# One more seven-product block in the first FFN slab pair that has any, and in each sweep of the FFN's last product

## The chip, the cores and the metric

The kernel is one program on one core of a Trainium2 chip. The metric is device time in microseconds (us); lower is better. Engines are named as in the profile: PE (matrix products), DVE (elementwise), ACT (elementwise and functions), POOL and SP (here mostly issuers of DMA). "Lnnn" is a line of the kernel.

## The reference

One decoder layer for 256 rows of width 2048, all in fp32:

```python
mod = silu(c) @ ada_w + ada_b          # six vectors: sh1, sc1, g1, sh2, sc2, g2
h   = rms_norm(x) * (1 + sc1) + sh1
u, lru_gate, q, k, v, mix_gates = split(h @ w_in + b_in)
y_lru  = rg_lru(conv(u)) * gelu(lru_gate)
y_attn = sliding_window_attention(q, k, v, sinks)
merged = gate_lru * (y_lru @ w_lru_out) + gate_attn * (y_attn @ w_attn_out)
x  = x + g1 * (merged @ w_o)
h2 = rms_norm(x) * (1 + sc2) + sh2
gate, up = split(h2 @ w_ffn_in)        # hidden size 5632
x  = x + g2 * ((silu(gate) * up) @ w_ffn_out)
out = rms_norm(x) * final_g
```

## The kernel before

**Products.** Every weight is read once, in 512 KB tiles `raw` of 128x1024. A weight tile is split in two: ACT casts it to `hi` (L330), DVE subtracts, `lo = raw - hi` (L342). A product of fp32 accuracy is then three matmuls, hi x hi, lo x hi and hi x lo (`mm3`, L382 to L384; in the plain blocks of the last sweeps L1391).

**Items.** All weights of the layer stand in one list, `items`, one tile each. `step(i)` does the products of item i; ahead of them it issues, for later items, the load of item i+5 (SP's queue; five `raw` buffers), `hi` of item i+3 (four buffers) and `lo` of item i+2 (three buffers). Whatever else DVE and ACT have to do (the posts of a finished block, the steps of side jobs) is written between these by a planner that keeps an estimated clock. The order on each engine is thus fixed when the program is built.

**Quads: plain and seven.** A quad is a pair of k-tiles (2 x 128 rows of the weight) by 1024 output columns. Done plainly it is two items and 24 matmuls. `seven()` does the same quad as a 2x2 block product with seven products instead of eight, 21 matmuls and four items: two raw tiles of it (here l0, of which half is used, and l1), and two sums of weight blocks, `wx` and `wy`. `wx` is loaded by POOL (`fill`, two DMAs of 256 KB, L443) and then a second block is added to it by two accumulating DMAs (`add`, L447); `step(i)` issues the fill for item i+15 and the add for item i+10. `wy` is two DVE additions (L458, L459). The seven products go to PSUM banks that all sevens of a slab or sweep share (`p`, `q`, `r`, `u`) and to the banks of the plain results. When the last of them is done, DVE adds the shared banks into the result.

The activations need sums as well. For the FFN's first product the sums of x are made in `second_norm` (`hs`, L477 to L480, L1186). For the second they are made slab by slab in `f_parts` (L1228; `fc` and `fs` for a slab that has a k-tile pair in `SEVEN`, `parts_of` with `fl`, L991, for one that has none), and in the sweep `al` is subtracted from them (`parts_low`, L1409).

**The stages that the change touches**, in order of time:
- `w_o`, four slabs of 512 columns, whose last post (`o_post`, L1120 to L1122) ends in the second RMSNorm;
- FFN in: 11 slab pairs (gate and up, 512 columns each) of eight quads. Slab pair 0 is plain, the others have sevens at the places that a string of turns gives ("7" is a seven, "-" a plain quad), at the k-tiles `SEVEN_1`;
- FFN out, sweep 1 (`w_f2a`, output columns 0 to 1023; k-tiles 0 to 35 by `TURNS`, then eight plain k-tiles) and sweep 2 (`w_f2d`, columns 1024 to 2047; k-tiles 0 to 35). `SEVEN` lists the k-tiles at which a sweep has a seven. After sweep 2 the last eight k-tiles of columns 1024 to 2047 follow in eight more items, and the residual, the second half of the final norm and the stores (`late`, L1461 to L1575).

**A side job.** `ada` makes the modulation vectors: SP loads a tile `aw`, DVE multiplies and sums it (L532). `ada_to(3, 4)` runs it until sh2 and sc2 are complete. `hold_sides` sets the planner's slack so low that no side job runs until `second_norm` is written.

Of the kernel before, what the change touches and what calls it, by code (L numbers as in the profile page):

```python
# [64 lines left out]
N_MADE, N_HOLD = 5, 4  # L65

N_SUM = (16, 11)
SEVEN = tuple(range(6, 36, 4))

SEVEN_1, SLAB_7 = (4, 6, 10, 12), 1  # L70

SLAB_G = 4
TURNS_1 = {1: "---7-77-"}

TURNS = "--7-7-7-7-7-7-7-7-"
EARLY = NH - 2 * N_HOLD

N_SPARE = 5
# [5 lines left out]
def hybrid_layer(  # L84
# [21 lines left out]
    def b4(name, dt=F32, shape=(4, S)):  # L106
        used["b4"] += 1
        return bp.tile([P, *shape], dt, tag="b4", name=name)
# [6 lines left out]
    def sum_bank(name):  # L115
        return ps.tile([P, 512], F32, tag="bank", name=name)
# [178 lines left out]
    items = []  # L295
# [397 lines left out]
    for i in range(N_PIECES):  # L693
        for n in range(N_F if i == 0 else 0, len(START)):
            s, k0, k1 = START[n], ends[i][n], ends[i + 1][n]
# [8 lines left out]
    def ada_to(*ms):  # L704
        while not {(m, kt) for m in ms for kt in range(NK)} <= cols_done:
            if not ada.advance():
                clock["pe"] += 1
                halves.fetch()
# [339 lines left out]
    def load_rows(s):  # L1048
        def before():
            xr.append(b4(f"xr{s}", F32, (2, 512)))  # L1050
            nc.sync.dma_start(xr[s], x_r[:, s * 512:(s + 1) * 512].rearrange("(t p) n -> p t n", p=P))
            if s == 3:
                ada_to(3, 4)
        return before

    def keep_rows(s):
# [29 lines left out]

    def hold_sides():

        clock["slack"] = -1e9
        return 0, 0  # L1090

    items[-2].before.append(hold_sides)

    def turn(p, of_w=False):

# [132 lines left out]
    def f_parts(s, pts):  # L1228

        seven_ = [j for j in range(2) if 4 * s + 2 * j in SEVEN]  # L1230
        if not seven_:
# [22 lines left out]
    def add_pair(s):  # L1254
# [54 lines left out]
        start = len(items)  # L1309
        turns = TURNS_1.get(s, "--77-77-")  # L1310
        sevens = SEVEN_1[:turns.count("7")]
# [43 lines left out]
    def bank(t, n):  # L1355

        if (t, n) not in fin:
            fin[t, n] = sum_bank(f"pf{t}{n}")
        return fin[t, n]
# [39 lines left out]
    def seven_last(k, n, src):  # L1399
        parts = {}  # L1400

        def parts_high():
            hi = parts[0] = b4(f"ah{n}_{k}", F32R, (8, P))
            nc.scalar.copy(hi[:, 0:7, :], f_sum[k][:, 0:7, :])
            return 0, 0.9

        def parts_low():
            lo = parts[1] = b4(f"al{n}_{k}", F32R, (8, P))
            nc.vector.tensor_tensor(lo[:, 0:7, :], f_sum[k][:, 0:7, :], f32(parts[0][:, 0:7, :]), op=ALU.subtract)  # L1409
            return 1.0, 0  # L1410

        def own(to):
            if to not in "pqru":
                return bank(int(to[0]), n + int(to[1]))
            if k == SEVEN[0]:
                fin[to] = sum_bank(f"p{to}{n}")
            return fin[to]

        items[-3].before.append(parts_high)
        items[-2].before.append(parts_low)  # L1420
        seven(
            (src[k], src[k + 1]), lambda j, i: src[k + j][:, i * 512:(i + 1) * 512], True,
            lambda a: [parts[h][:, a, :] for h in range(2)], own, k == SEVEN[0], k == SEVEN[-1],
            (lambda: combined(n)) if k == SEVEN[-1] else None,
        )

    def combined(n):

        v = [b4(f"v{n}{i}", F32, (2, 512)) for i in range(2)]
        pq, pqu, pqr, pqur = v[0][:, 0, :], v[0][:, 1, :], v[1][:, 0, :], v[1][:, 1, :]  # L1430
        nc.scalar.copy(pq, fin["p"])

        def add(t, j, x):
            y = sp.tile([P, 512], F32, tag="t2", name=f"yv{n}{t}{j}")
            x2 = x2_of(t, (n + j) * 512, (n + j + 1) * 512)
            nc.vector.tensor_tensor(y, x, g2_of((n + j) * 512, (n + j + 1) * 512), op=ALU.mult)
            nc.vector.tensor_tensor(x2, y, x2, op=ALU.add)

        yield 0, 0.6
        add(0, 0, pq)  # L1440
        nc.vector.tensor_tensor(pq, fin["q"], pq, op=ALU.add)
        yield 1.8, 0
        nc.vector.tensor_tensor(pqu, fin["u"], pq, op=ALU.add)
        nc.vector.tensor_tensor(pqr, fin["r"], pq, op=ALU.subtract)
        nc.vector.tensor_tensor(pqur, fin["r"], pqu, op=ALU.subtract)
        yield 1.8, 0
        add(0, 1, pqr)
        yield 1.2, 0
        add(1, 0, pqu)
        yield 1.2, 0  # L1450
        add(1, 1, pqur)
        free(b4=2)
        yield 1.2, 0
        if n == 2:
            yield from early_rows()
# [38 lines left out]
    for n, src in ((0, w_f2a), (2, w_f2d)):  # L1494
        start = len(items)
        kinds = {"7": iter(SEVEN), "-": iter(k for k in range(0, EARLY, 2) if k not in SEVEN)}
        turns = [next(kinds[c]) for c in TURNS]
        for k in turns + list(range(EARLY, NH if n == 0 else EARLY, 2)):
            if k in SEVEN:
                seven_last(k, n, src)  # L1500
# [244 lines left out]
```

## Time and profile before

| what | value |
|---|---|
| time, median of 3 runs | 1537.02 us (1536.7 to 1537.57) |
| the profiled execution: its own time | 1538.73 us |
| its span, first to last instruction | 1537.0 us |
| mean granted TensorE clock | 0.998 |
| busy: PE / DVE / ACT / POOL | 99% / 89% / 57% / 11% of the span |
| DMA | 444.58 MB, mean 289 GB/s |

The span is what the trace covers; the time of the same execution is 1.73 us longer. In the trace a row gives the start of an instruction in us from the span's start, its duration, its engine and line, and, in square brackets, how long the engine sat idle before it and what ended that. Durations of instructions that follow each other overlap a little, since the ends are drawn with the pipeline's latency; what an instruction costs its engine is the distance from its start to the next one's.

### The profile page before, as it was taken

The numbers are of one execution on the slowest core, as the hardware profiler recorded it, in microseconds if no ns is written. First come the engines' busy times: TensorE is split into PE (matmuls) and PEld (weight loads), VectorE is DVE, ScalarE is ACT, GpSimd is POOL, SyncE is SP. The second block draws the span as 40 slices with busy tenths as digits, with TensorE's granted clock in tenths as the row PEclk, the third lists the DMA queues.
The fourth block names the chain that finished last, engine by engine and source line by source line (L and its number), as shares of the span: only waits on it lengthen the run. The fifth ranks groups of instructions, "written<-read, shape, count | busy, mean of one in ns | idle before, by whom it ended". The sixth has DMA issues, their size and how long they took to land.

```text
span 1537.0 us, 20204 instructions
## 1 busy us (share of the span) xinstructions
PE 1521.0 (99%) x6851; PEld 1249.0 (81%) x6851; DVE 1365.3 (89%) x1835; ACT 880.7 (57%) x1142; POOL 163.5 (11%) x232
## 2 busy tenths in 40 slices
PE   8999999999999999999999999999999999999997
PEld 5788888888888787888887878888888888888886
DVE  7999999888898888988988899999999999888987
ACT  4654444886964446444444556656665556664664
POOL 0000000000000000000002231034212122321200
PEclk9999999999999999999999999999999999999999
DMA  9999988656786887999999999589898979989983
GB/s 368 383 345 362 345 315 301 207 181 217 241 286 226 291 308 283 364 325 341 377 373 347 312 338 273 167 254 332 274 273 248 269 243 298 288 257 297 275 266 124
DMA packets 138440, 444.58 MB, mean 289 GB/s; under 512 B 16064, under 2 KB 16224, under 8 KB 138336
## 3 DMA queue, kind: packets, MB, share of 16 engines
q1 hardware_dynamic: 113056, 384.02, 70.2%
q0 software_dynamic: 24992, 58.75, 16.1%
q8 instruction: 53, 0.87, 0.2%
q10 hardware_dynamic: 288, 0.52, 0.1%
q14 instruction: 51, 0.42, 0.1%
HBM read 439.02 MB, written 4.21 MB: 288 GB/s over the span
## 4 chain that ended last, share of the span: by engine, by line
PE 93%; DMA 3%; DVE 3%; ACT 0%; issue 0%; SPq 0%; DVEq 0%; ACTq 0%
PE pf L1391 10%; PE f L383 6%; PE f L382 6%; PE f L384 6%; PE wi L383 6%; PE wi L384 6%; PE wi L382 6%; PE wl L384 2%; PE wl L383 2%; PE wga L384 2%; PE wl L382 2%; PE wga L382 2%; PE wgl L383 2%; PE wga L383 2%; PE wgl L384 2%; PE wa L384 2%
## 5 line engine op out<-in xcount | busy, mean ns | idle before, releaser
L330 ACT CAST hi<-raw 128x1024 fp32r<-128x1024 f32 (+1 forms) x540 | 532.3, 996 | 419.1 <-PE wi L384 87.4
L342 DVE TENSOR_TENSOR lo<-raw,hi 128x1024 fp32r<-128x1024 f32 (+1 forms) x540 | 611.9, 1149 | 82.1 <-issue 37.7
L383 PE MATMUL wi<-lo,h 128*128 128x512 f32 x432 | 168.4, 390 | 3.3 <-DVE lo L342 3.3
L382 PE MATMUL wi<-hi,h 128*128 128x512 f32 x432 | 169.9, 393 | 0.0
L384 PE MATMUL wi<-hi,h 128*128 128x512 f32 x432 | 168.2, 389 | 0.0
L382 PE MATMUL f<-hi,h 128*128 128x512 f32 x406 | 158.8, 391 | 0.0
L383 PE MATMUL f<-lo,h 128*128 128x512 f32 x406 | 158.1, 389 | 0.0
L384 PE MATMUL f<-hi,h 128*128 128x512 f32 x406 | 158.0, 389 | 0.0
L532 DVE CUSTOM_DVE_ANT_0 aw<-aw,crow,vec 128x1024 f32<-128x1024 f32 x95 | 120.5, 1277 | 6.0 <-DMA aw<-in_ada_t_dram 6.0
L532 DVE CUSTOM_DVE_ANT_0 aw<-aw,crow,modc 128x1024 f32<-128x1024 f32 x95 | 121.1, 1277 | 1.6 <-DMA aw<-in_ada_t_dram 1.6
L330 ACT CAST hi<-wy 128x1024 fp32r<-128x1024 f32 x55 | 58.0, 1055 | 74.3 <-PE f L384 32.1
L383 PEld LDWEIGHTS wi<-lo,h 128*128 128x128 f32 x432 | 81.1, 188 | 20.9 <-DVE lo L342 4.3
L342 DVE TENSOR_TENSOR lo<-wx,hi 128x1024 fp32r<-128x1024 f32 x55 | 67.2, 1222 | 32.4 <-issue 28.5
L330 ACT CAST hi<-wx 128x1024 fp32r<-128x1024 f32 x55 | 58.0, 1055 | 64.8 <-PE pf L1391 24.0
L382 PEld LDWEIGHTS wi<-hi,h 128*128 128x128 f32 x432 | 81.1, 188 | 16.8 <-ACT acc L611 0.2
L384 PEld LDWEIGHTS wi<-hi,h 128*128 128x128 f32 x432 | 81.1, 188 | 16.7
L384 PEld LDWEIGHTS f<-hi,h 128*128 128x128 f32 x406 | 76.2, 188 | 15.8
L383 PEld LDWEIGHTS f<-lo,h 128*128 128x128 f32 x406 | 76.2, 188 | 15.7 <-DVE lo L342 0.3
L382 PEld LDWEIGHTS f<-hi,h 128*128 128x128 f32 x406 | 76.2, 188 | 15.6
L447 POOL DMA_DIRECT2D wx<-in_w_f_dram x78 | 69.8, 969 | 79.5 <-DMA wx<-in_w_f_dram 78.4
L443 POOL DMA_DIRECT2D wx<-in_w_f_dram x78 | 44.7, 627 | 287.6 <-DVE lo L342 95.2
L342 DVE TENSOR_TENSOR lo<-wy,hi 128x1024 fp32r<-128x1024 f32 x55 | 67.2, 1222 | 6.9 <-ACT hi L330 4.3
(347 smaller groups left out, 3094.1 us busy)
## 6 DMA issues: line engine op xcount, KB each, us to landing
aw<-in_ada_t_dram SPq DMA_DIRECT2D x190, 512.0 KB, 6.7
raw<-in_w_in_dram SPq DMA_DIRECT2D x164, 512.0 KB, 5.1
raw<-in_w_f_dram SPq DMA_DIRECT2D x137, 512.0 KB, 6.5
wx<-in_w_f_dram POOLq DMA_DIRECT2D x156, 256.0 KB, 7.9
raw<-in_w_f2a_dram SPq DMA_DIRECT2D x36, 512.0 KB, 6.4
raw<-in_w_lru_dram SPq DMA_DIRECT2D x32, 512.0 KB, 4.6
raw<-in_w_att_dram SPq DMA_DIRECT2D x32, 512.0 KB, 5.5
raw<-in_w_o_dram SPq DMA_DIRECT2D x32, 512.0 KB, 8.1
```

What stands on the lines that cost most here:

```text
L330: nc.scalar.copy(hi[:, cs], live[i][0][:, cs])
L342: nc.vector.tensor_tensor(lo[:, cs], raw[:, cs], f32(hi[:, cs]), op=ALU.subtract)
L382: nc.tensor.matmul(ps, lhsT=lh, rhs=rh, start=start, stop=False, skip_group_check=True)
L383: nc.tensor.matmul(ps, lhsT=lh, rhs=rl, start=False, stop=False, skip_group_check=True)
L384: nc.tensor.matmul(ps, lhsT=ll, rhs=rh, start=False, stop=stop, skip_group_check=True)
L443: nc.gpsimd.dma_start(x[:, j * 512:(j + 1) * 512], block(0, 1))
L447: nc.gpsimd.dma_start(got["x"][:, j * 512:(j + 1) * 512], block(j, j), accum_op=ALU.add)
L532: nc.vector.tensor_tensor_reduce(out=r, in0=r, in1=crow[j], op0=ALU.mult, op1=ALU.add, scale=1.0, scalar=dst if j else vec[:, v:v + 1], ac ...
L1391: nc.tensor.matmul(bank(t, n), lhsT=l[:, rows(t)], rhs=w[:, c0:c0 + 512], start=kt == 0 and k == 0, stop=kt == (EARLY - 2 if (t, n) == (1, ...
```

## The change

Three constants change, and the call `ada_to(3, 4)` with the place of `hold_sides`:

```diff
-SEVEN = tuple(range(6, 36, 4))
+SEVEN = tuple(range(2, 36, 4))
 
 SEVEN_1, SLAB_7 = (4, 6, 10, 12), 1
...
-TURNS_1 = {1: "---7-77-"}
-
-TURNS = "--7-7-7-7-7-7-7-7-"
+TURNS_1 = {}
+
+TURNS = 9 * "-7"
...
             nc.sync.dma_start(xr[s], x_r[:, s * 512:(s + 1) * 512].rearrange("(t p) n -> p t n", p=P))
-            if s == 3:
-                ada_to(3, 4)
         return before
...
     def hold_sides():
 
+        ada_to(3, 4)
         clock["slack"] = -1e9
         return 0, 0
 
-    items[-2].before.append(hold_sides)
+    items[-3].before.append(hold_sides)
```

- **Slab pair 1** had three sevens of eight quads, in the turns `---7-77-`; without an entry in `TURNS_1` it gets the turns that slab pairs 2 to 10 have, `--77-77-`, with four.
- **Each sweep** had eight sevens of 18 quads and has nine. A sweep now begins plain, seven and ends with a seven (of its k-tiles 0 to 35), where it began plain, plain, seven and ended with a plain quad. The new seven is at k-tiles 2 and 3, so slab pair 0 now makes `fc` and `fs` in `f_parts` instead of `fl`.
- **`ada_to(3, 4)`** stood at the first item of the last `w_o` slab; it now stands at that slab's last item but two, in `hold_sides`, one item earlier than `hold_sides` was.

What this does to the order of instructions shows at three places. First, DVE at the end of `w_o`. `lo_6925` to `lo_6964` are the splits of the first tiles of FFN in, `aw` is a step of `ada`, and `yo` begins the last post of `w_o`. Before:

```order
L532 ISA aw_6864,modc<-aw_6864,crow_108,vec 128x1024
...
L342 TENSOR_TENSOR lo_6925<-raw_6858,hi_6902 128x1024
L532 ISA aw_6886,modc<-aw_6886,crow_108,vec 128x1024
...
L342 TENSOR_TENSOR lo_6946<-raw_6880,hi_6923 128x1024
L342 TENSOR_TENSOR lo_6964<-raw_6900,hi_6944 128x1024
L1120 TENSOR_TENSOR yo_7008<-wo_0_0_6821,g_6095 128x512
```

After (the numbers in the names shift by one, the lines too):

```order
L532 ISA aw_6864,modc<-aw_6864,crow_108,vec 128x1024
...
L342 TENSOR_TENSOR lo_6925<-raw_6858,hi_6902 128x1024
L342 TENSOR_TENSOR lo_6945<-raw_6880,hi_6923 128x1024
L342 TENSOR_TENSOR lo_6963<-raw_6900,hi_6943 128x1024
L1119 TENSOR_TENSOR yo_7007<-wo_0_0_6821,g_6095 128x512
```

The step `aw_6886` has left this place; it stands some 40 rows further down, in FFN in. Second, POOL's queue from the same time on, with the `wx` tiles of slab pair 1. Before:

```order
L443 DMA wx_7291<-in_w_f1_dram 128x512 x2
L447 DMA wx_7291<-in_w_f1_dram 128x512 x2
L443 DMA wx_7432<-in_w_f1_dram 128x512 x2
L443 DMA wx_7542<-in_w_f1_dram 128x512 x2
L447 DMA wx_7432<-in_w_f1_dram 128x512 x2
```

After:

```order
L443 DMA wx_7246<-in_w_f1_dram 128x512 x2
L443 DMA wx_7339<-in_w_f1_dram 128x512 x2
L447 DMA wx_7246<-in_w_f1_dram 128x512 x2
L447 DMA wx_7339<-in_w_f1_dram 128x512 x2
L443 DMA wx_7479<-in_w_f1_dram 128x512 x2
```

Two fills now stand ahead of the first add. Third, DVE at the start of sweep 2, where the residual of sweep 1 (`y` and `x`, four pairs) is worked off between the splits. Before:

```order
L1461 TENSOR_TENSOR y_0_12264<-pf_11293,g_12033 128x512
...
L342 TENSOR_TENSOR lo_12271<-raw_12207,hi_12248 128x1024
L1461 TENSOR_TENSOR y_0_12289<-pf_11301,g_12033 128x512
...
L342 TENSOR_TENSOR lo_12295<-raw_12228,hi_12269 128x1024
L1461 TENSOR_TENSOR y_512_12311<-pf_11295,g_12033 128x512
...
L342 TENSOR_TENSOR lo_12317<-raw_12246,hi_12293 128x512
L1409 TENSOR_TENSOR al_6_12321<-fs_7918,ah_6_12297 128x896
L1461 TENSOR_TENSOR y_512_12335<-pf_11303,g_12033 128x512
...
L458 TENSOR_TENSOR wy<-wx,raw_12267 128x512
```

After:

```order
L1460 TENSOR_TENSOR y_0_12298<-pf_11312,g_12082 128x512
...
L342 TENSOR_TENSOR lo_12303<-raw_12244,hi_12280 128x512
L1408 TENSOR_TENSOR al_2_12307<-fs_7537,ah_2_12284 128x896
L1460 TENSOR_TENSOR y_0_12325<-pf_11320,g_12082 128x512
...
L458 TENSOR_TENSOR wy<-wx,raw_12262 128x512
...
L342 TENSOR_TENSOR lo_12336<-raw_12262,hi_12301 128x1024
L1460 TENSOR_TENSOR y_512_12353<-pf_11314,g_12082 128x512
...
L342 TENSOR_TENSOR lo_12361<-wx,hi_12334 128x1024
L1460 TENSOR_TENSOR y_512_12367<-pf_11322,g_12082 128x512
...
L342 TENSOR_TENSOR lo_12375<-wy,hi_12359 128x1024
```

The first seven's half split, `al` and `wy` now stand among the residual pairs, where two whole splits of plain tiles stood (the second row of each pair is left out above).

## The prediction

> **What bounds the kernel now.** First the page's busy times and its shares of the chain that ended last:
>
> ```profile
> PE 1521.0 (99%) x6851; PEld 1249.0 (81%) x6851; DVE 1365.3 (89%) x1835; ACT 880.7 (57%) x1142; POOL 163.5 (11%) x232
> PE 93%; DMA 3%; DVE 3%; ACT 0%; issue 0%; SPq 0%; DVEq 0%; ACTq 0%
> ```
>
> PE is the bound nearly everywhere, so fewer matmuls are a gain of their full length. But DVE is at 89% over the whole span, and a seven takes matmuls from PE by giving DVE sums. So the question at each place is whether DVE, or a DMA before it, is then still in time. Next the chain itself, in order of time (start, us):
>
> ```profile
> 809.21 13.02 DMA raw<-in_w_f_dram
> 822.32 1.06 ACT hi L330
> 823.44 1.11 issue
> 824.54 0.70 DVE yo L1120
> ...
> 1298.32 5.44 PE pf L1391 x24
> 1303.77 0.87 PE ft L982 x8
> 1304.64 5.46 PE pf L1391 x24
> 1314.86 5.44 PE pf L1391 x24
> ...
> 1386.26 38.08 PE pf L1391 x168
> ...
> 1500.49 21.76 PE pf L1391 x96
> ```
>
> A plain quad is 24 matmuls in 5.44 us, 0.2267 each; 168 of them in 38.08 give the same. The chain leaves PE where w_o joins FFN in (809 to 824): there a load that took 13 us, its cast, and a post of DVE set the time. In the sweeps it runs on PE without a break.
>
> **Arithmetic.** One seven more in slab pair 1 and one more in each sweep: three quads of 21 matmuls instead of 24, 9 x 0.2267 = **-2.04 us**. This is all that the change can win by matmuls, 0.13%. Under 0.2% (3.07 us) this kernel's measurement can't tell a difference from none; so faster or slower is decided by the waits at five places.
>
> **Place 1, the join of w_o and FFN in.** DVE, ACT and POOL there:
>
> ```profile
> 820.63 1.28 DVE L532 CUSTOM_DVE_ANT_0 aw<-aw,crow,vec 128x1024 f32<-128x1024 f32 x1 [2.02 <-DMA aw<-in_ada_t_dram]
> ...
> 823.40 1.23 DVE L342 TENSOR_TENSOR lo<-raw,hi 128x1024 fp32r<-128x1024 f32 x1 [0.34 <-ACT hi L330]
> ```
>
> ```profile
> 824.88 1.05 ACT L330 CAST hi<-raw 128x1024 fp32r<-128x1024 f32 x1 [1.51 <-DMA raw<-in_w_f_dram]
> 825.99 0.63 ACT L1122 ACTIVATE yo<-xr 128x512 f32<-128x512 f32 x1
> ```
>
> ```profile
> 812.86 1.08 POOL L443 DMA_DIRECT2D wx<-in_w_f_dram  x2 [93.06 <-PE wo L384]
> ...
> 823.51 1.12 POOL L443 DMA_DIRECT2D wx<-in_w_f_dram  x2 [1.08 <-PE wo L384]
> ```
>
> The step `aw` at 820.63 is the one that moves away. It buys nothing: the last split before the post (823.40) waits for the cast at 822.32, and that for the load issued at 809.21. DVE idles 0.34 us before it already, and would only idle longer. The step's own 1.21 us fall due in FFN in (place 2).
>
> On POOL a second fill now stands ahead of the first add. Before, POOL reached it at 823.51, held by the end of w_o. After, its buffer is one that w_o's last slab gives back two items after the first fill's: 812.86 + 2 x 2.72 (half a plain quad) = 818.3. So 512 KB are asked for 5 us earlier. What such a fill does to the loads in flight, by the DMA queues from 817 to 820 us (first fill under way) and from 821 to 824 (none):
>
> ```profile
> q1 hardware_dynamic: 203, 0.75, 61.6%
> q0 software_dynamic: 140, 0.47, 39.2%
> ```
>
> ```profile
> q1 hardware_dynamic: 336, 1.22, 102.2%
> ```
>
> SP's loads (q1) get 0.75 MB in 3 us beside POOL's queue (q0), and 1.22 MB alone. The Trainium skill ("DMA: Bandwidth & Descriptors", Queues, rings and completion order) says that each DMA engine takes turns between the queues it has work for, a packet at a time; the trace agrees, with 39% and 62%. The first fill was issued at 812.86 and moved most of its 0.5 MB from 817 on, some 4 us later; the second, issued at 818.3, would move from 822.3. It then meets the load that ended at 824.88 (the cast's idle of 1.51 us ended with it): 2.6 us at 0.75/1.22 instead of full rate, about 1.0 us lost. ACT casts that tile directly before the squares of the norm (L1122, 825.99), which are on the path to h2. So 0 (if its packets come after 824.9) to +1.4 us; I take **+1.0**.
>
> **Place 2, slab pair 1.** Durations on DVE, and DVE's waits there:
>
> ```profile
> 874.04 1.22 DVE L342 TENSOR_TENSOR lo<-raw,hi 128x1024 fp32r<-128x1024 f32 x1
> ...
> 880.06 1.23 DVE L342 TENSOR_TENSOR lo<-raw,hi 128x1024 fp32r<-128x1024 f32 x1 [1.08 <-ACT hi L330]
> ...
> 890.92 0.68 DVE L458 TENSOR_TENSOR wy<-wx,raw 128x512 f32<-128x512 f32 x1
> ...
> 892.25 0.68 DVE L342 TENSOR_TENSOR lo<-raw,hi 128x512 fp32r<-128x512 f32 x1
> 892.85 1.28 DVE L532 CUSTOM_DVE_ANT_0 aw<-aw,crow,modc 128x1024 f32<-128x1024 f32 x1
> ...
> 894.06 0.28 DVE L477 TENSOR_TENSOR hs<-x1T 128x128 f32<-128x128 f32 x1
> ...
> 894.99 1.22 DVE L342 TENSOR_TENSOR lo<-wx,hi 128x1024 fp32r<-128x1024 f32 x1
> 896.12 1.22 DVE L342 TENSOR_TENSOR lo<-wy,hi 128x1024 fp32r<-128x1024 f32 x1
> ```
>
> ```profile
> 895.81 0.39 PE L382 MATMUL fr<-hi,hs 128*128 128x512 f32 x1
> 896.26 0.50 PE L383 MATMUL fr<-lo,hs 128*128 128x512 f32 x1
> 896.60 0.40 PE L384 MATMUL fr<-hi,hs 128*128 128x512 f32 x1
> ```
>
> ```profile
> 890.00:910.00 20.00, 19.93 (x88) 15.89 (x87) 18.99 (x26) 11.05 (x13) 8.79 (x13) 1.00 1.07 309
> ```
>
> By distances of starts a split costs 1.13 us (894.99 to 896.12), a half split 0.60, `wy` 1.33 (890.92 to 892.25), an `ada` step 1.21, four `hs` sums 0.93. A plain quad is then 2.26 us of DVE, a seven 0.60 + 1.33 + 3 x 1.13 = 5.32, against 4.76 us of PE (21 x 0.2267): a seven alone already outruns PE. From 890 to 910 DVE is busy 18.99 of 20 us (third pair of numbers after the window's length), and PE already waits for the split of `wx` (895.81 to 896.60 is 0.79 us for two steps of 0.227, 0.34 lost; some 0.9 in the whole slab pair).
>
> The change adds to DVE +3.06 (5.32 - 2.26), +1.21 (the moved step), and +0.3 since slab pair 0's post makes `fc` and `fs` (0.60 + 0.93) instead of two `fl` (1.2). The first seven starts one quad earlier, before DVE has any lead. Counting on from 874.04 in the order of the changed kernel, with the wait for the raw tile at 880.06 kept, DVE ends the split of the first `wx` at 892.1; PE wants it at 890.6, so it waits 1.5. The same count gives 0.5, 0.5, 1.1 and 0.3 at the next tiles of the two sevens: 3.9 in place of 0.9, **+3.0**. Bounds: +0.9 if the loads come 1 to 2 us earlier than in the trace (the idle of 1.08 is then DVE's to use), +4.5 if they come later by the 0.5 MB more that a seven loads (0.5 MB is 1.2 us at 1.22 MB in 3 us).
>
> **Place 3, start of sweep 1**, and **place 4, start of sweep 2**, on DVE:
>
> ```profile
> 1301.87 2.95 DVE L342 TENSOR_TENSOR lo<-raw,hi 128x1024 fp32r<-128x1024 f32 x3
> 1304.75 1.08 DVE L1409 TENSOR_TENSOR al<-fs,ah 128x896 fp32r<-128x896 f32 x1
> ...
> 1411.91 0.69 DVE L1461 TENSOR_TENSOR y<-pf,g 128x512 f32<-128x512 f32 x1 [0.31 <-PE pf L1391]
> ...
> 1413.24 1.22 DVE L342 TENSOR_TENSOR lo<-raw,hi 128x1024 fp32r<-128x1024 f32 x1
> ```
>
> Sweep 1: DVE is occupied with the last slab's post until 1301.87. Now no second plain quad (5.44 PE, 2.26 DVE) comes before the seven: half split 0.60, `al` 1.0, `wy` 1.33, split 1.13, two more splits, and only then the two `fl` of the last slab (0.60 each), to 1309.4. The seven's products `u` and `q` go to banks that hold the last slab's transposes until these `fl`. So the seven, which could run from 1304.64 to 1309.40, ends at 1310.9: **+1.5** (0 if the banks turn out free, +2 if the raw tiles are late too).
>
> Sweep 2: sweep 1 ends on PE at 1386.26 + 5 x 5.44 = 1413.46. Before, four residual pairs of 1.33 each (1411.91 to 1413.24) lay beside two plain quads; now beside one plain and a seven. Counted on from 1411.91: DVE ends the split of `wy` at 1423.6 where PE wants it at 1422.5: **+1.1** (0 to +2).
>
> **Place 5, the end.**
>
> ```profile
> 1529.11 0.29 DVE L1461 TENSOR_TENSOR y<-late,g 128x128 f32<-128x128 f32 x1 [1.30 <-PE late L384]
> ```
>
> After the last seven (1500.49) one plain quad less follows: PE has 5.44 us less to do, DVE, which has to add the shared banks and the residuals, only 2.26 less. These 3.2 us are covered by the 1.30 us that DVE waits for PE here and by what it waits for ACT before that (0 to 1.3): **+1.6**, between +0.5 and +2.
>
> **Sum.** -2.04 + 1.0 + 3.0 + 1.5 + 1.1 + 1.6 = +6.2; the 1.0 at the join also gives the loads of slab pair 1 time, so some 0.7 of it is counted twice: **+5.4**. Against the profiled execution 1538.73 + 5.4 = 1544.1; that execution lies 1.71 above the median of the runs, 1537.02, so against that 1542.4. The low bounds give -2.04 + 0.9 + 0.5 = -0.6, 1536.4; the high ones +9.9, 1546.9, which would need all of them at once.
>
> **Rivals.**
> - *Part of the waits is hidden.* Only slab pair 1 and one more place, or only the sweeps and the tail cost: +0 to +3, 1537 to 1540. For it: DVE still has idle time in these stretches (1.08 at 880), and one wait absorbs the next.
> - *All hidden:* -2.04, 1535.0. For it: the chain is on PE through both sweeps. Against it: the seven's 5.32 us on DVE per 4.76 on PE, with nothing ahead of it at three places.
> - *The join gets faster (the other side).* If without `aw` the loads queued on SP behind its buffer are issued sooner, the cast at 822.32 moves up and the post no longer stands the 1.11 us from 823.44 to 824.54. With all else hidden, -2.04 - 1.11 = -3.15, 1533.9. It decides from 0.3 us of such a gain with every other place at nothing. Against it: the load in question was issued 11 us before `aw` ran.
> - *The clock drops.* In these windows (the third number from the end is the granted clock)
>
> ```profile
> 50.00:54.00 4.00, 2.26 (x11) 1.54 (x10) 2.95 (x4) 3.97 (x8) 0.00 (x0) 1.00 1.03 410
> ...
> 830.00:834.00 4.00, 4.00 (x18) 3.63 (x17) 3.46 (x9) 2.08 (x5) 2.85 (x4) 0.61 1.04 409
> ```
>
> PE was idle 1.7 of 4 us once and kept the full clock (50 to 54), and it ran at 0.61 for 4 us right behind the join. A wait like the join's elsewhere could cost 0.39 x 4 = 1.6 us more: with the sum 1544.0, and with the higher terms above 1545. The waits forecast here are at most 1.5 us each, shorter than the one at 50, so I expect no drop. The Trainium skill ("TensorE: Matmul & The Clock Gate", Part 1) has the clock halve after an idle window of about 3.4 us, and no wait in these rows is as long as that.
>
> **Chances.** The forecast (waits at four or five places, 1541 to 1544.5): 0.50. Part hidden: 0.28. All hidden: 0.09. Faster join: 0.07. Above 1545: 0.06. Faster by over 0.2% (below 1533.9) 0.07; within 0.2% 0.37; slower (above 1540.1) 0.56. The range 1534.8 to 1545.0 leaves out the last two; the likeliest case alone is 1540.5 to 1544.5.
>
> **What will show it.** The join: `yo` L1119 at 824.5 still, the cast before the squares later by 1 us, the second fill on POOL near 818. Slab pair 1: PE waiting 1 us or more at the first split of `wx` near 890, DVE without idle from 880 to 915. Sweeps: PE idle released by `fl` near 1310, by DVE near 1422. End: no idle released by `late` on DVE. The prediction is wrong if the loads in slab pair 1 come earlier than in this trace, if the banks are free in time, or if the post at the join moves.

## The result and the profile after

The changed kernel takes 1546.05 us (median of 6 runs, 1545.31 to 1548.31), the kernel before 1536.86 in the same runs: ratio 1.0061, 95% interval 1.0048 to 1.0074, some 9.2 us slower. The forecast was 1542.4 with a range to 1545.0: the direction was right, the size too small.

Page of the changed kernel, the busy times (1.):

```profile
PE 1520.9 (99%) x6842; PEld 1247.6 (81%) x6842; DVE 1376.4 (89%) x1852; ACT 886.8 (57%) x1151; POOL 172.3 (11%) x244
```

PE has nine matmuls fewer and DVE 11 us more than before (1365.3). Where the time goes shows best by stages, cut at the starts of matmuls in the trace: the first `fg` (FFN in begins), the first `ft` of the posts of slab pairs 0, 1 and 2, the first `pf` (sweep 1), the first and the last `late`. The stages left out of the table, slab pairs 3 to 10, take 330.6 to 331.1 in every execution. All profiled executions of this study, in us:

| kernel | first `fg` at | slab pair 0 | 1 | 2 | sweeps | after last matmul | span |
|---|---|---|---|---|---|---|---|
| before | 831.86 | 50.14 | 43.51 | 42.02 | 223.93 | 8.17 | 1536.97 |
| before, second profile | 833.16 | 49.66 | 43.07 | 42.02 | 223.93 | 8.19 | 1537.48 |
| before, third profile | 830.39 | 49.65 | 44.02 | 42.03 | 223.93 | 8.18 | 1536.04 |
| **changed** | 830.02 | 49.64 | **48.43** | 42.22 | **225.99** | **9.95** | 1543.65 |
| changed, second profile | 831.63 | 49.65 | 48.28 | 42.20 | 226.85 | 9.93 | 1545.92 |
| `ada` | 828.79 | 49.68 | 47.02 | 42.01 | 223.93 | 8.17 | 1536.91 |
| `slab1` | 829.81 | 49.66 | 45.60 | 41.97 | 223.93 | 8.18 | 1536.63 |
| `sweeps` | 830.07 | 49.66 | 43.41 | 42.01 | 225.93 | 9.90 | 1538.49 |
| `sweeps`, second profile | 832.11 | 49.63 | 43.44 | 42.07 | 225.99 | 9.92 | 1541.03 |
| `noadd1` | 830.67 | 49.67 | 45.68 | 42.26 | 226.27 | 9.91 | 1541.87 |
| `nosides1` | 829.42 | 49.66 | 43.40 | 43.70 | 227.19 | 9.93 | 1540.83 |
| `ends` | 830.32 | 49.66 | 43.43 | 42.00 | 227.44 | 8.18 | 1538.38 |
| `best` | 830.16 | 49.66 | 43.35 | 43.02 | 227.91 | 8.20 | 1539.63 |
| `ada_noadd1` | 829.14 | 49.68 | 46.18 | 42.03 | 223.93 | 8.20 | 1536.80 |

From the first `fg` to the end the three profiles of before take 705.1, 704.3 and 705.7 us, the two of the changed kernel 713.6 and 714.3: +8.9, and that is nearly the +9.2 of the medians. It is slab pair 1 (+4.8), the sweeps (+2.1 to +2.9) and the tail (+1.8).

Slab pair 1 of the changed kernel, on PE and DVE:

```profile
888.23 0.40 PE L382 MATMUL fr<-hi,hs 128*128 128x512 f32 x1
892.13 0.79 PE L383 MATMUL fr<-lo,hs 128*128 128x512 f32 x1 [3.50 <-DVE lo L342]
892.72 0.63 PE L384 MATMUL fr<-hi,hs 128*128 128x512 f32 x1
...
897.41 0.49 PE L383 MATMUL fp<-lo,h 128*128 128x512 f32 x1
```

```profile
884.38 1.28 DVE L532 CUSTOM_DVE_ANT_0 aw<-aw,crow,vec 128x1024 f32<-128x1024 f32 x1 [2.23 <-DMA aw<-in_ada_t_dram]
...
885.59 0.68 DVE L458 TENSOR_TENSOR wy<-wx,raw 128x512 f32<-128x512 f32 x1
...
887.52 1.28 DVE L532 CUSTOM_DVE_ANT_0 aw<-aw,crow,vec 128x1024 f32<-128x1024 f32 x1
...
890.86 1.22 DVE L342 TENSOR_TENSOR lo<-wx,hi 128x1024 fp32r<-128x1024 f32 x1
```

The same by windows (length, busy time of PE, PEld, DVE, ACT and POOL, granted clock, share of DMA time, GB/s):

```profile
888.00:892.00 4.00, 0.62 (x3) 0.19 (x1) 3.96 (x10) 2.02 (x4) 0.88 (x1) 0.85 1.04 402
892.00:897.00 5.00, 4.87 (x12) 3.81 (x13) 4.93 (x10) 2.20 (x3) 3.92 (x6) 0.50 1.08 297
```

At the split of the first `wx` PE waits 3.5 us, where it waited 0.2 before. DVE comes to that split late because, at 884, it had stood 2.2 us in front of an ada step whose tile had not landed, and everything behind that step on DVE's queue stood with it. The third view has what follows: from 892 to 897 PE runs at half clock. The rows from 892.13 to the matmul after 897.41, fourteen steps, take 5.6 us instead of 3.2.

Starts of the sweeps, PE's waits between 1300 and 1500 us (waiting engine, line, releaser, us in total, times, longest); the same view of the kernel before has no line:

```profile
PE pu L382 <- DVE fl L991: 0.9, 1, 0.9
PE pq L383 <- DVE lo L342: 0.8, 1, 0.8
PE pf L383 <- DVE lo L342: 0.5, 1, 0.5
```

And the end, on DVE:

```profile
1533.21 0.16 DVE L1529 RECIPROCAL r<-r 128x1 f32<-128x1 f32 x1 [0.36 <-ACT r L1520]
...
1534.47 0.55 DVE L1460 TENSOR_TENSOR y<-late,g 128x384 f32<-128x384 f32 x1
...
1535.53 0.28 DVE L1460 TENSOR_TENSOR y<-late,g 128x128 f32<-128x128 f32 x1
```

DVE no longer waits for PE's last products (1.30 us before); PE's last matmul starts at 1533.70, and DVE comes to it at 1535.53.

### The profile page after: what moved, and what is told of

Its sections match the earlier page's. It is cut to its first block, busy times and chain, and to the rows that moved or that the text cites. A ratio compares the mean times of both kernels' runs of the same rounds, so it can differ in the third digit from the quotient of the medians.

```text
span 1543.7 us, 20263 instructions
## 1 busy us (share of the span) xinstructions
PE 1520.9 (99%) x6842; PEld 1247.6 (81%) x6842; DVE 1376.4 (89%) x1852; ACT 886.8 (57%) x1151; POOL 172.3 (11%) x244
## 5 line engine op out<-in xcount | busy, mean ns | idle before, releaser
L382 PE MATMUL f<-hi,h 128*128 128x512 f32 x400 | 156.8, 392 | 0.0
L384 PE MATMUL f<-hi,h 128*128 128x512 f32 x400 | 155.9, 390 | 0.0
L330 ACT CAST hi<-wy 128x1024 fp32r<-128x1024 f32 x58 | 61.1, 1054 | 80.5 <-PE f L384 32.0
L342 DVE TENSOR_TENSOR lo<-wx,hi 128x1024 fp32r<-128x1024 f32 x58 | 70.9, 1222 | 32.2 <-issue 28.8
L330 ACT CAST hi<-wx 128x1024 fp32r<-128x1024 f32 x58 | 61.2, 1056 | 65.0 <-PE pf L1390 25.3
L447 POOL DMA_DIRECT2D wx<-in_w_f_dram x80 | 71.6, 955 | 87.4 <-DMA wx<-in_w_f_dram 79.3
L1390 PE MATMUL pf<-hi,fc 128*128 128x512 f32 x288 | 79.9, 389 | 0.0
L342 DVE TENSOR_TENSOR lo<-wy,hi 128x1024 fp32r<-128x1024 f32 x58 | 70.9, 1222 | 7.9 <-ACT hi L330 4.9
```

The lines of the kernel that those rows point to most:

```text
L330: nc.scalar.copy(hi[:, cs], live[i][0][:, cs])
L342: nc.vector.tensor_tensor(lo[:, cs], raw[:, cs], f32(hi[:, cs]), op=ALU.subtract)
L382: nc.tensor.matmul(ps, lhsT=lh, rhs=rh, start=start, stop=False, skip_group_check=True)
L384: nc.tensor.matmul(ps, lhsT=ll, rhs=rh, start=False, stop=stop, skip_group_check=True)
L447: nc.gpsimd.dma_start(got["x"][:, j * 512:(j + 1) * 512], block(j, j), accum_op=ALU.add)
L1390: nc.tensor.matmul(bank(t, n), lhsT=l[:, rows(t)], rhs=w[:, c0:c0 + 512], start=kt == 0 and k == 0, stop=kt == (EARLY - 2 if (t, n) == (1, ...
```

## The experiments

**1. One part alone** (three kernels), and the kernel before again.

`ada`:

```diff
-            if s == 3:
-                ada_to(3, 4)
...
+        ada_to(3, 4)
         clock["slack"] = -1e9
...
-    items[-2].before.append(hold_sides)
+    items[-3].before.append(hold_sides)
```

> Only the call ada_to(3, 4) and hold_sides move; turns and SEVEN as before. If the moved ada step is what let the join start its post 2 us earlier in the changed kernel, yo starts near 822.5 here too and the first matmul of FFN in near 830 instead of 831.9: about -1.5 us against the profiled execution of before. If the join's place differs only from execution to execution (the theory of the prediction: the step buys nothing), yo starts at 824.5 and the time is within 0.5 us of before.

Measured: ratio 1.0017 (1.0009 to 1.0026), +2.6 us: slower, which neither theory had. The profiled execution has an early join (`fg` at 828.79) and loses it in slab pair 1, 47.0 us instead of 43.5. The step that left the join pushes each later ada step back by one place, and two of them now stand in the second seven of slab pair 1, on DVE:

```profile
900.26 1.28 DVE L532 CUSTOM_DVE_ANT_0 aw<-aw,crow,modc 128x1024 f32<-128x1024 f32 x1
...
902.80 0.68 DVE L342 TENSOR_TENSOR lo<-raw,hi 128x512 fp32r<-128x512 f32 x1
903.40 1.27 DVE L532 CUSTOM_DVE_ANT_0 aw<-aw,crow,modc 128x1024 f32<-128x1024 f32 x1
904.60 1.22 DVE L342 TENSOR_TENSOR lo<-wx,hi 128x1024 fp32r<-128x1024 f32 x1
```

PE waits there, and loses clock behind it (its waits, and the window after):

```profile
PE fr L383 <- DVE lo L342: 1.4, 1, 1.4
PE f L383 <- DVE lo L342: 1.1, 1, 1.1
```

```profile
904.00:910.00 6.00, 4.62 (x15) 3.39 (x14) 5.97 (x9) 2.55 (x4) 1.07 (x2) 0.72 1.08 314
```

`slab1`:

```diff
-TURNS_1 = {1: "---7-77-"}
+TURNS_1 = {}
```

> Only slab pair 1 gets its fourth seven; the ada step and both sweeps as before. Theory A (slab pair 1 itself, with its late loads, makes most of the loss): a wait of 3 us or more at the first split of wx near 890, then several us at a lower clock; in all +4 to +7 us. Rival B (it needs the ada step that was moved into this stretch): wait of at most 1.5 us, no clock loss, +1 to +2.5 us.

Measured: ratio 1.0020 (1.0011 to 1.0029), +3.1 us, and slab pair 1 takes 45.6. No wait as long as the one of the whole change, and no loss of clock: rival B in kind, a little above its numbers. PE waits at the tiles of two sevens, as the prediction counted, 2.4 us in all:

```profile
PE fr L383 <- DVE lo L342: 1.9, 2, 1.1
PE f L383 <- DVE lo L342: 0.3, 1, 0.3
PE fp L383 <- DVE lo L342: 0.2, 1, 0.2
```

So slab pair 1's loss has two parts that each cost 2 to 3.5 us alone, the seven and the ada step, and 4.8 together.

`sweeps`:

```diff
-SEVEN = tuple(range(6, 36, 4))
+SEVEN = tuple(range(2, 36, 4))
...
-TURNS = "--7-7-7-7-7-7-7-7-"
+TURNS = 9 * "-7"
```

> Only the sweeps have nine sevens, starting plain, seven and ending on a seven. By the two traces PE loses 1.9 us at the start of sweep 1 and 1.4 at the start of sweep 2, wins 1.4 by fewer matmuls, and the tail behind the last matmul is 1.8 longer: +3.7 us. Slab pair 1 keeps three sevens and PE waits there under 1 us; slab pair 0's post with fc and fs costs nothing seen there. If the sweeps' waits come only from being late after slab pair 1, it is -1.4.

Measured: ratio 1.0031 (1.0019 to 1.0042), +4.8 us, where the traces show +2.0 in the sweeps and +1.7 in the tail; 3.7 lies inside the interval. The waits are there without any delay from slab pair 1, so they are the sweeps' own.

`again`, without an edit:

> The kernel before, once more, for the place of the join from execution to execution. If the profiled execution of before was an unlucky one, the first matmul of FFN in starts earlier than 831.9 here, the granted clock right behind it stays at 1.00, and the span is 1 to 2 us shorter; if the join is the same in each execution, span and join agree within 0.3 us.

Measured: `fg` at 833.16, later still, and a time of 1539.26, while 22 runs of the same kernel without a profile lay between 1535.14 and 1537.43 on that chip. What differs is told below, with the third profile.

**2. What makes the loss in slab pair 1.** `noadd1` is the changed kernel with

```diff
+                if s == 1:
+                    items[-2].sums = items[-2].sums[0], lambda: None
```

> The changed kernel, where slab pair 1 leaves out the eight accumulating DMAs (L447): wx is one weight block instead of a sum of two, everything on DVE, ACT and PE is as in the changed kernel. The measure is the time from the first matmul of FFN in to the transposes of slab pair 1's post: 93.7 us before, 98.1 in the changed kernel. If late loads make the loss (DVE stands 2.2 us at an ada step whose tile is late, and what it has to do comes after), 94 to 95.5 us here and the time 3 us below the changed kernel's. If DVE's amount of work makes it, 97 us or more, within 1 us of the changed kernel.

Measured: slab pair 1 takes 45.68, 2.75 us less than in the changed kernel (the 93.7 and 98.1 of the expectation are the sums with slab pair 0; here 95.35), and the time is 1543.12 (ratio 1.0046, 1.0031 to 1.0062). DVE takes the ada tile at 882.05 without a wait, PE's longest wait is 0.8, and the clock stays at 1.00:

```profile
882.05 1.28 DVE L532 CUSTOM_DVE_ANT_0 aw<-aw,crow,vec 128x1024 f32<-128x1024 f32 x1
```

```profile
PE fr L383 <- DVE lo L342: 1.6, 3, 0.8
PE f L383 <- DVE lo L342: 0.3, 1, 0.3
PE fp L383 <- DVE lo L342: 0.2, 1, 0.2
```

```profile
886.00:890.00 4.00, 3.30 (x15) 2.45 (x14) 3.96 (x10) 2.90 (x4) 1.77 (x2) 1.00 1.02 400
```

So the long wait and the half clock behind it, 2.75 us net, are made by DMA: without these accumulating transfers the tile is in time. They don't run in slab pair 1 itself. In the changed kernel POOL issues them from 821.6 to 853.9 us, for the `wx` tiles that slab pair 1 will use; those for slab pair 2 (from 867.4 on) stay in `noadd1`. What reaches the tile at 884 is then a backlog: from 860 to 866 us the share of DMA time (second from the end; it can come out a little above 1) is 1.05 in the changed kernel and 0.90 in `noadd1`:

```profile
860.00:866.00 6.00, 6.00 (x28) 4.99 (x27) 5.35 (x7) 2.13 (x3) 0.26 (x1) 1.00 1.05 361
```

```profile
860.00:866.00 6.00, 6.00 (x28) 4.99 (x27) 5.06 (x7) 3.14 (x5) 0.85 (x2) 1.00 0.90 320
```

The other 2.1 us stay, as in `slab1` (45.60). In neither is a tile of the side job late by more than 0.8 us, so what is left goes with DVE's amount of work, as the prediction counted it.

`nosides1` is the changed kernel with

```diff
+        if s in (1, 2):
+            items[start].before.append(lambda: slack_to(-1e9 if s == 1 else SLACK[1]))
...
```

(`slack_to` sets the planner's slack; at -1e9 no side job is written.)

> The changed kernel, but no ada step is written while slab pair 1 runs; the five that stood there come in slab pair 2. If the ada steps (their 1.2 us each on DVE, their loads, the wait for them) are what the fourth seven collides with, the wait at the first split of wx falls under 1.5 us, the clock stays at 1.00 near 893, and the same stretch takes 93 to 94.5 us instead of 98.1: about 4 us below the changed kernel, +4 to +5 against before, which are the sweeps and the tail. If the fourth seven alone is too much for DVE, 96 us or more.

Measured: slab pair 1 takes 43.40 and keeps its clock; slab pair 2, which now has the five ada steps, 43.70 instead of 42.0. Ratio 1.0046 (1.0033 to 1.0058), about 2.4 us less than the changed kernel where about 4 were expected: 5.0 back in one slab pair, 1.5 lost in the next, 1.2 more in the sweeps of that execution (227.19; 0.8 of it at some plain products near 1397 to 1404, for which no cause was sought). The ada steps, by their work or by their loads, which both left, are the other half of the collision. But even so four sevens in 43.4 us are no shorter than three in 43.1 to 44.0: the 0.68 us of matmuls is taken by waits that remain.

`ada_noadd1` is `ada` with the edit of `noadd1`:

> The kernel with only the ada step moved, where slab pair 1 also leaves out its six accumulating DMAs (wx is one weight block instead of a sum). With them slab pair 1 took 47.0 us from post to post, 43.3 before. If the moved step costs by the loads that come later behind it (ACT waits for raw tiles at 894 to 899), 43 to 44.5 us here; if by its 1.2 us on DVE, 46 us or more.

Measured: slab pair 1 takes 46.18, against 47.02 with the accumulating transfers, inside the case "by its 1.2 us on DVE". PE's wait at the second `wx` and the half clock behind it are still there (903.33 to 905.11 is 1.78 us, less one step 1.55):

```profile
903.33 0.40 PE L382 MATMUL fr<-hi,hs 128*128 128x512 f32 x1
905.11 0.61 PE L383 MATMUL fr<-lo,hs 128*128 128x512 f32 x1 [1.38 <-DVE lo L342]
905.51 0.63 PE L384 MATMUL fr<-hi,hs 128*128 128x512 f32 x1
```

The run can't separate the two cases, though. The six transfers left out are issued from 818.0 to 835.9 us in `ada`, some 60 us before that wait, and the loads of the raw tiles near 894 to 899 are no earlier without them: ACT still waits 1.33, 1.53 and 0.82 us for them (0.92, 1.54 and 1.05 in `ada`). That the step's place carries most of the loss in `ada` is likely, since it stands directly ahead of the split for which PE waits and takes 1.21 us there, but it isn't shown.

**3. Is it the ninth seven, or where the first and the last stand?** `ends` and `best` are made from the kernel before:

```diff
-SEVEN = tuple(range(6, 36, 4))
+SEVEN = tuple(range(2, 36, 4))
...
-TURNS = "--7-7-7-7-7-7-7-7-"
+TURNS = "--7-7-77-7-7-77-7-"
```

> The kernel before with nine sevens in each sweep, but the sweep begins plain, plain, seven and ends with a plain quad (turns --7-7-77-7-7-77-7-); slab pair 1 and the ada step as before. If the sweeps lose only by where the first and the last seven stand, the waits at the two starts and the longer tail are gone and two quads of three matmuls less are left: -1.4 us (-2 to 0). If a ninth seven is too much for DVE wherever it stands, or two sevens in a row are, +1 to +4.

Measured: ratio 1.0023 (1.0014 to 1.0033), +3.5 us; the second case of the expectation. The tail is back at 8.18 us and no wait is left at the starts. But there are now two places in each sweep with a seven directly behind a seven, and each costs 1.1 us by starts of matmuls (four waits of PE in the same view as above, 1300 to 1500 us):

```profile
PE pf L383 <- DVE lo L342: 3.4, 4, 0.9
```

A seven of a sweep takes DVE 6.3 us (the prediction's 5.32 and `al`, 1.0) against 4.76 of PE, so it falls 1.5 behind, and the plain quad ahead of it (2.26 against 5.44) is what makes up for that. Nine sevens with a plain quad ahead of each fill the 18 quads and leave none for the start or the end; the eight of before leave one for each.

`best` adds to `ends` the fourth seven in slab pair 1 and the edit of `nosides1`:

> The kernel before with the fourth seven in slab pair 1 and no ada step there, and with the sweeps of the run beside it that begin with two plain quads and end with one; the ada step at the join as before. If both losses are placement, three quads of three matmuls less are left: -2.0 us (-3 to 0). If the fourth seven is too much for DVE even so, +0.5 to +2.

Measured: ratio 1.0038 (1.0025 to 1.0050), +5.6 us, above both cases of the expectation. Slab pair 1 takes 43.35, slab pair 2 43.02, the sweeps 227.91: neither part gives its matmuls back. No kernel here beats the one before.

**4. From execution to execution.** `again2` is the kernel before, `sweeps_again` the kernel `sweeps`, `after_again` the changed kernel, each profiled once more:

> The kernel before, a third profile. Both profiles so far have the first matmul of FFN in at 831.9 and 833.2 and times above all the other runs of it on the chip; all seven kernels built from it have it at 828.8 to 830.7. If the two were unlucky executions, this one can lie at 829 to 830.5 with a span near 1534 to 1535; if the kernel before has the late join whenever it is profiled, 831.5 to 833.5 again.

> The kernel with nine sevens in the sweeps and nothing else changed, once more; up to the join it has the instructions of the kernel before. If the place of the join varies from execution to execution, the first matmul of FFN in lies anywhere from 829 to 833; the sweeps take 225.9 us and the tail behind the last matmul 9.9 us as in its first profile, whatever the join does.

> The changed kernel, a second profile. If its stages are fixed and only the join varies from execution to execution, slab pair 1 takes 48 to 49 us from post to post with PE waiting 3 us or more at the first split of wx and a lower clock behind it, the sweeps 226.0, the tail 9.9, while the first matmul of FFN in lies anywhere from 829 to 833. If the late ada tile near 884 was chance, slab pair 1 takes 45.5 to 46.5.

Measured: `fg` at 830.39, 832.11 and 831.63. Three executions of before spread over 2.8 us at this place, two of `sweeps` over 2.0, two of the changed kernel over 1.6. But in the last two pairs the difference lies ahead of the join: the last matmul of `w_o` already starts 2.5 us later in `sweeps_again` (826.06 against 823.58; its granted clock was 0.946, against 0.996) and 1.4 later in `after_again` (824.88 against 823.47). The join itself, from that matmul to the first `fg`, takes 8.8, 9.5 and 6.9 us in before, 6.5 and 6.1 in `sweeps`, which has the same instructions up to there, 6.55 and 6.75 in the changed kernel, and 5.7 to 7.3 in the others. What moves in before is when the last raw tiles of the join land. ACT's casts, in its second and third profile:

```profile
823.23 1.05 ACT L330 CAST hi<-raw 128x1024 fp32r<-128x1024 f32 x1 [3.57 <-DMA raw<-in_w_f_dram]
825.78 1.05 ACT L330 CAST hi<-raw 128x1024 fp32r<-128x1024 f32 x1 [1.51 <-PE pt L1100]
```

```profile
821.30 1.05 ACT L330 CAST hi<-raw 128x1024 fp32r<-128x1024 f32 x1 [3.48 <-DMA raw<-in_w_f_dram]
824.54 1.05 ACT L330 CAST hi<-raw 128x1024 fp32r<-128x1024 f32 x1 [2.19 <-DMA raw<-in_w_f_dram]
```

Slab pair 1 of the changed kernel took 48.43 and 48.28, and DVE waited 2.23 and 2.21 us for the same ada tile, so that wait is no chance. Its sweeps are less fixed than expected: 225.99 and 226.85, with PE's first wait there 1.1 us in place of 0.5.

## Why the prediction was wrong in size, step by step

- **Arithmetic, -2.04.** In the trace as matmuls; none of it is left as time in any kernel.
- **The join, +1.0: not seen.** The second fill did come early (POOL has it at 818.72, forecast 818.3):

```profile
818.72 1.07 POOL L443 DMA_DIRECT2D wx<-in_w_f_dram  x2 [4.59 <-PE wo L384]
```

  But the cast before the squares came at 824.17 (824.88 in the profile of before), `yo` at 822.54 instead of 824.5, and `slab1`, which has the same early fill, has `fg` at 829.81. All of this lies inside the 2.8 us by which before itself moves. The step took one execution's join for the kernel's. Six executions with the early fill take 5.7 to 7.3 us from the last `w_o` matmul to `fg`, the eight without it 5.7 to 9.5. That the moved ada step "buys nothing" agrees with them: 5.7 is reached with the step in its old place (`best`) and without it (`ada`). The deduction of some 0.7 that leads from +6.2 to +5.4 rests on this join and falls with it.
- **The step against the median.** I put the profiled execution 1.71 us above the median and let that cancel. It doesn't: three profiled executions of before (1538.73, 1539.26, 1537.82) all lie above the runs without a profile made beside them, by 1.9 to 3.3 us, the changed kernel's (1545.42 and 1547.68) lie among its other runs. What makes a profiled execution of before longer wasn't tried; a late join is what two of the three traces show.
- **Slab pair 1, +3.0 of waits: the term that was mis-sized.** Forecast net of the seven's own 0.68: +2.3; measured +4.8. The count of DVE's work came close: `slab1` and `noadd1`, in which no tile of the side job is late by more than 0.8 us, lose 2.1 to 2.2 us. The step that failed was the bound "+4.5 if they come later by the 0.5 MB more that a seven loads". It priced lateness by the bytes of the loads that the seven adds (1.2 us), spread over several tiles. The late tile was one of the side job, and it held the head of DVE's queue for 2.2 us; PE's wait became 3.5 us in one piece. The moved step was priced at its 1.21 us on DVE alone, although the prediction's own row at 820.63 shows such a step standing 2.02 us for its tile, and of the expected signs "DVE without idle from 880 to 915" failed for the same reason.
- **The clock: nothing was put in the sum.** "The waits forecast here are at most 1.5 us each" was the reason, and it fell with that wait: half clock for some 5 us, 2.4 us lost. Not all of it is extra: the waits that `noadd1` has behind the first one (1.2 us) don't occur here, so that the late tile and the clock together cost 2.75. Forecast as a rival with 0.06 and 1.6 us.
- **Sweep 1, +1.5, sweep 2, +1.1.** Right in place and mechanism: the split behind `wy` (0.5), the bank that waits for `fl` (0.9), the split of `wy` among the residual pairs (0.8); by starts of matmuls 1.9 and 1.4. Each was short by 0.3 to 0.4, since PE also loses a few tenths around each wait.
- **The end, +1.6.** Measured +1.8, with DVE's wait for `late` gone as forecast.

Sum without the join: forecast +5.2 (6.2 - 1.0), measured +8.9 behind the join; 2.5 of the missing 3.7 are slab pair 1.

## What to carry to other kernels

- Price an in-order engine's wait by what stands behind it: a side job's step that stood 2.2 us for its tile in front of the critical split made a PE wait of 3.5 us in place of 0.7, and then half clock. Where a stage is short of both DVE and DMA, look which side steps the order puts there before adding work, and which transfers are queued tens of us before.
- A product scheme that saves matmuls needs a cheaper block ahead of each dear one: count the elementwise time per block against the matmul time per block, and the first and the last block by what stands around them.
- Profile the kernel before twice. A stage that moves by 2.8 us between executions of the same instructions can carry no term of 1 us.

## What the runs showed of the hardware

- The TensorE clock fell to 0.50 for about 5 us behind a wait of 3.5 us. That agrees with the rule quoted in the prediction from the Trainium skill ("TensorE: Matmul & The Clock Gate", Part 1: half clock after an idle window of about 3.4 us). But shorter waits were followed by half clock too (matmuls 0.43 us apart): one of 3.0 us in `after_again`, 1 us after it had ended; two of 1.1 and 1.4 us within 4 us in `ada` (0.72 from 904 to 910); and in `ada_noadd1` one of 1.4 us with one of 0.2 ahead of it (0.72 as well). In `slab1`, with waits up to 1.1 us, it stayed at 1.00, and so it did behind the single wait of 1.7 us in the prediction's window from 50 to 54. So a wait well under 3.4 us can cost clock; the measurement decides here. Which of the short ones do is not shown, for their length alone doesn't tell 1.4 from 1.7.
- An accumulating transfer took the DMA engines about twice as long as a plain one, by the bytes that the trace counts. In the changed kernel from 874 to 882 us, while POOL's queue (q0) mostly moved accumulating transfers, it moved 0.88 MB in 59.5% of the engines' time, SP's loads (q1) 1.43 MB in 49.0%:

```profile
q0 software_dynamic: 479, 0.88, 59.5%
q1 hardware_dynamic: 473, 1.43, 49.0%
```

  For the same time that is half as much. With a plain fill on POOL's queue, in the prediction's window from 817 to 820, the two queues are equal: 0.47 MB in 39.2% and 0.75 in 61.6%. By this the transfers that `noadd1` leaves out weigh about twice their bytes.
